# Norm statistics, norm and first projections of a stage by token segment in a one-core transformer program

## The chip, the cores and the metric

One core of one Trainium2 chip runs the whole program. The metric is the device time of one execution in microseconds: 2895.19 us as the median of three runs of the kernel before (2885.41 to 2896.55). Less is better.

## What is computed

Two transformer blocks of two and three layers run one after the other over 256 tokens of `x` and 256 tokens of a context `ctx`, width 1024. Every layer has a mixer and a feed-forward part, and each is entered through the same three steps: an RMS norm over the 1024 features, a scale and a shift that come from a modulation vector, and a projection. Each ends with an output projection that is added to `x` (and to the context) through a gate. In the reference this is:

```python
def rms_norm(x, g):
    xf = x.astype(jnp.float32)
    y = xf * lax.rsqrt(jnp.mean(xf * xf, axis=-1, keepdims=True) + EPS)
    return (y * g.astype(jnp.float32)).astype(x.dtype)
...
        hx = modulate(rms_norm_2(x, norm_ffn_g[i]), mod_x[3], mod_x[4])
        x = x + mod_x[5] * squared_relu_ffn(hx, ffn_w1[i], ffn_w2[i])
        if with_ctx_out:
            ctx = ctx + mod_c[2] * yc
            hc = modulate(rms_norm_2(ctx, norm_ffn_g[i]), mod_c[3], mod_c[4])
            ctx = ctx + mod_c[5] * squared_relu_ffn(hc, ffn_w1[i], ffn_w2[i])
```

The first block's mixers are a mixture of Fourier mixing, differential attention, neighbourhood attention and a gated MLP, followed by a convolutional feed-forward part. The second block's mixers are a gated delta rule, gated linear attention and plain attention, followed by a squared-ReLU feed-forward part.

## The kernel before

Activations lie with the features on the partitions: `xT` and `cT` are [128, 8, 256], feature 128k + p in partition p of slice k, one column a token. They stay in SBUF. A tile of 512 columns holds x's tokens in columns 0 to 255 and the context's in 256 to 511; these two halves are called segments. Every f32 operand is split into a high and a low part, and a product is three matmuls: high by high, low by high, high by low (`mm3`, L144 to L146). The weights come as [128, 1024] blocks by DMA into `raw`; ACT copies the high part (`whi`, L132) and POOL, or now and then DVE, subtracts it for the low part (`wlo`, L135). Two pairs of them rotate in one pool, and a third lies in the stage's own pool.

The stages, with the seams between them in the trace: start → mixer 0 (to 61 us), mixer 0 → FFN 0 (343), FFN 0 → mixer 1 (742), mixer 1 → FFN 1 (about 940), FFN 1 → delta mixer (1180), delta → ffn2(0) (2057), ffn2(0) → gla mixer (2425), gla → ffn2(1) (2690). FFN 1 and ffn2(1) have x only.

A seam consists of these pieces. `out_proj` (L666, for FFN stages) and `out_pair` (L800, for mixers) compute the eight output tiles of 128 features, 512 columns at a time. DVE adds each tile through the gate to `xT` and then to `cT` (L675, L811), and after a tile they call `stats`' step (L615 to L651) for the slice two tiles back, after the last tile for the last ones. A step squares the slice on ACT for x and for the context (L633); steps 1 to 5 are summed on DVE into `nsum` (L647); the sum, step 6 and step 7 go through matmuls with a matrix of ones that add over the partitions (L638, L635); then ACT takes Ln for both segments and Exp for both (L642, L645), which gives the reciprocal root. Ln and Exp each have an `ACT_TABLE_LOAD` before them. `norm_mod` (L651) makes from it the normed input of the next stage, slice by slice: on DVE `nt` = x · gain · `nsum` (L662), on ACT the high part `hh` = `nt` + shift (L663), on DVE the low part `hl` (L664). `nt` has two buffers. It goes over the eight slices, with the two segments inside. `first_fm` (L160), the mixers' `mix_first` (items at L1000) and the delta mixer's own list (L1479) send the next stage's first two or three projections through `mm3_lag` (L156 to L158), which takes slice after slice, all the items in each, the third item three slices later, so that PE can follow the norm while it goes on.

At the seams generators for the modulation vectors run in between (`mod_part`, L533). They either sum weight blocks `graw` by DVE into `gacc` (L547, L549) or take them through small matmuls (`bank_pm`, L552), then copy the result on ACT (`modt`, L564) and transpose it (L567).

The order on each engine is set by a scheduler that goes by the order of the code and by its own estimate of when operands are there. Each stage takes its tiles from pools that are opened at its start; their memory is that of the stage before, so that a first write into a new stage's tile waits for the last use of the old one.

## Time and profile before

| what | value |
|---|---|
| median of three runs | 2895.19 us (2885.41 to 2896.55) |
| profiled execution, its own time | 2895.47 us |
| its span, first to last instruction | 2893.7 us |
| mean granted TensorE clock | 0.972 of full speed |
| PE busy | 94%, 18,780 matmuls |
| PE weight loads busy | 72% |
| DVE, ACT, POOL busy | 60%, 45%, 35% |
| HBM read | 330.69 MB, 115 GB/s over the span |

The profile is that of one execution. Busy time of PE is counted from a matmul's start to its modelled end, and successive matmuls overlap, so the spacing of their starts is what a matmul costs in a dense stretch. The granted clock tells how much of the full speed of 2.4 GHz the chip gave TensorE in a stretch; the low level is 1.2 GHz.

### The profile page before, as it was taken

The page shows a single profiled execution, that of the slowest core. Times are in us where ns is not written, and L with a number is a line of the kernel's source. Part 1 is how long each engine was busy: PE and PEld are TensorE (multiplying, and loading weights), DVE is VectorE, ACT ScalarE, POOL GpSimd, SP SyncE. Part 2 cuts the span into 40 slices and gives each one's busy share as a digit, 9 for nine tenths or more (in the row PEclk, how much of TensorE's full clock was granted, in tenths as well). Part 3 has the DMA queues.
Part 4 walks back from the last instruction along what each step waited for, and adds up shares of the span by engine and source line. Part 5 has one row for each costly group of instructions (what it writes and reads, how often), then busy time and mean ns, then how long its engine had stood idle before and what let it go on. Part 6 is the DMA issues. An engine that isn't in the chain of part 4 may idle for free. (4 is left out here: it accounts for less than half of the span.)

```text
span 2893.7 us, 47135 instructions
## 1 busy us (share of the span) xinstructions
PE 2721.3 (94%) x18780; PEld 2085.7 (72%) x18780; DVE 1725.8 (60%) x3440; ACT 1302.6 (45%) x2287; POOL 1013.5 (35%) x565
## 2 busy tenths in 40 slices
...
GB/s 307 124 107 55 150 155 182 153 156 117 202 108 110 212 223 219 131 66 31 30 38 38 37 45 38 45 38 37 104 191 179 95 97 114 126 74 30 124 184 160
DMA packets 92567, 334.79 MB, mean 116 GB/s; under 512 B 10267, under 2 KB 10779, under 8 KB 91708
## 3 DMA queue, kind: packets, MB, share of 16 engines
...
HBM read 330.69 MB, written 1.05 MB: 115 GB/s over the span
## 5 line engine op out<-in xcount | busy, mean ns | idle before, releaser
L135 POOL TENSOR_TENSOR wlo<-raw,whi 128x1024 fp32r<-128x1024 f32 (+1 forms) x349 | 845.7, 2425 | 1732.8 <-ACT whi L132 1550.5
L132 ACT ACTIVATE whi<-raw 128x1024 fp32r<-128x1024 f32 (+1 forms) x418 | 437.3, 1046 | 691.9 <-PE bank_pj L145 429.6
L144 PE MATMUL bank_pj<-hh,whi 128*128 128x512 f32 (+1 forms) x1712 | 615.5, 360 | 1.7 <-DVE gz L1114 0.9
L146 PE MATMUL bank_pj<-hh,wlo 128*128 128x512 f32 (+1 forms) x1712 | 610.4, 357 | 5.6 <-POOL wlo L135 5.3
L145 PE MATMUL bank_pj<-hl,whi 128*128 128x512 f32 (+1 forms) x1712 | 609.0, 356 | 0.0
L146 PEld LDWEIGHTS bank_pj<-hh,wlo 128*128 128x128 f32 x1712 | 327.9, 192 | 62.0 <-issue 19.2
L144 PEld LDWEIGHTS bank_pj<-hh,whi 128*128 128x128 f32 x1712 | 327.9, 192 | 61.3 <-issue 23.3
L145 PEld LDWEIGHTS bank_pj<-hl,whi 128*128 128x128 f32 x1712 | 328.3, 192 | 49.0 <-issue 15.5
L549 DVE SCALAR_TENSOR_TENSOR gacc<-graw,sv,gacc 128x1024 f32<-128x1024 f32 x84 | 147.0, 1753 | 43.2 <-DMA graw<-in_ada_w 23.5
L144 PE MATMUL bank_pj<-f2h,whi 128*128 128x512 f32 (+1 forms) x512 | 172.5, 337 | 0.0
L145 PE MATMUL bank_pj<-f2l,whi 128*128 128x512 f32 (+1 forms) x512 | 171.2, 334 | 1.2 <-DVE f2l L175 1.2
L146 PE MATMUL bank_pj<-f2h,wlo 128*128 128x512 f32 (+1 forms) x512 | 171.9, 336 | 0.0
L175 DVE TENSOR_TENSOR f2l<-f2r,f2h 128x512 fp32r<-128x512 f32 (+1 forms) x64 | 66.5, 1044 | 126.9 <-ACT f2h L174 126.9
L144 PE MATMUL bank_pj<-acth,whi 128*128 128x512 f32 (+1 forms) x352 | 120.3, 343 | 7.9 <-ACT acth L174 7.9
L145 PE MATMUL bank_pj<-actl,whi 128*128 128x512 f32 (+1 forms) x352 | 119.0, 338 | 0.5 <-DVE actl L175 0.5
L146 PE MATMUL bank_pj<-acth,wlo 128*128 128x512 f32 (+1 forms) x352 | 119.1, 338 | 0.0
L675 DVE SCALAR_TENSOR_TENSOR xT<-bank_pj,m,xT 128x256 f32<-128x256 f32 x64 | 30.9, 483 | 141.7 <-PE bank_pj L146 141.6
L764 PE MATMUL bank_pj<-whi,hh 128*128 128x256 f32 x384 | 112.2, 292 | 1.3 <-DVE gck L1073 1.2
L764 PE MATMUL bank_pj<-wlo,hh 128*128 128x256 f32 x384 | 111.3, 290 | 1.4 <-POOL wlo L135 1.4
L764 PE MATMUL bank_pj<-whi,hl 128*128 128x256 f32 x384 | 111.0, 289 | 0.0
L552 PE MATMUL bank_pm<-graw,sv 128*32 128x256 f32 x896 | 81.9, 414 | 30.6 <-DMA graw<-in_w_ada 21.3
L145 PEld LDWEIGHTS bank_pj<-f2l,whi 128*128 128x128 f32 x512 | 96.0, 188 | 12.1 <-DVE f2l L175 1.4
...
## 6 DMA issues: line engine op xcount, KB each, us to landing
raw<-in_f SPq DMA_DIRECT2D x128, 512.0 KB, 3.7
graw<-in_w_ada SPq DMA_DIRECT2D x96, 512.0 KB, 4.5
graw<-in_ada_w SPq DMA_DIRECT2D x96, 512.0 KB, 4.5
raw<-in_up SPq DMA_DIRECT2D x88, 512.0 KB, 3.7
raw<-in_dn_w SPq DMA_DIRECT2D x48, 512.0 KB, 3.6
raw<-in_down SPq DMA_DIRECT2D x32, 512.0 KB, 3.6
raw<-in_win_fm SPq DMA_DIRECT2D x20, 512.0 KB, 3.8
raw<-in_win_tm SPq DMA_DIRECT2D x16, 512.0 KB, 5.1
```

The lines of the kernel that those rows point to most:

```text
L132: nc.scalar.activation(hi[:, :n], raw[:, :n], AF.Copy)
L135: eng.tensor_tensor(out=lo[:, :n], in0=raw[:, :n], in1=hi[:, :n].bitcast(F32), op=ALU.subtract)
L144: nc.tensor.matmul(out, lhsT=lh, rhs=rh, start=(idx == 0), stop=False)
L145: nc.tensor.matmul(out, lhsT=lh, rhs=rl, start=False, stop=False)
L146: nc.tensor.matmul(out, lhsT=ll, rhs=rh, start=False, stop=(idx == n - 1))
L175: nc.vector.tensor_tensor(out=lo, in0=src, in1=hi.bitcast(F32), op=ALU.subtract)
L549: nc.vector.scalar_tensor_tensor(out=acc[:, v], in0=raw, scalar=s[:, k, v:v + 1], in1=acc[:, v], op0=ALU.mult, op1=ALU.add)
L552: nc.tensor.matmul(ps[32 * j:32 * j + 32, :256], lhsT=s[:, k, :], rhs=raw[:, j * 256:(j + 1) * 256], start=first, stop=(k == 7 and direct ...
L675: nc.vector.scalar_tensor_tensor(out=x[:, mt], in0=ps[:, o:o + x.shape[2]], scalar=gate(vec, mt), in1=x[:, mt], op0=ALU.mult, op1=ALU.add)
L764: nc.tensor.matmul(out[i], lhsT=x, rhs=y, start=(a == 0 and kk == 0 and n == 0), stop=(a == 1 and kk == 3 and n == 2))
```

## The change

Segments get an order of their own at the seams, x's tokens first and the context's after them.

- `out_proj`: where statistics follow and there are two segments, the last three output tiles (5 to 7) are computed for x's 256 columns first, then for the context's; their three weight pairs are held meanwhile. `out_pair`: the second weight's four tiles (4 to 7) likewise.
- `stats`' step takes the segments it is for, and Squares, sums, ones matmuls, Ln and Exp are then made for those alone; Ln is one instruction over both where both are done together.
- `norm_mod` has the segments outside and the slices inside. A buffer `nt` is taken for one slice of one segment.
- The first projections run `mm3_lag` twice, over 256 columns of x and then of the context.

In all 463 matmuls of 512 columns become two of 256: 288 in first projections (72, 72, 24, 48 and 72 of them at the start, mixer 0 → FFN 0, FFN 0 → mixer 1, FFN 1 → delta and delta → ffn2(0)), 54 and 72 in output tiles of FFN 0 and ffn2(0), 24 + 24 in those of mixer 0 and delta. ACT gets eight more table loads, two at each of the four seams with two segments and statistics in the tiles. Outside of the seams the code is the same.

```diff
--- before.py
+++ after.py
@@ -153,17 +153,17 @@
...
     def first_fm(self, ws, h, T, tags, lags):
 
-        items = []
-        for (wh, wl), tag, lag in zip(ws, tags, lags):
-            items.append((self.bank(tag)[:, :T], [((wh[:, k], wl[:, k]), tuple(a[:, :T] for a in h(k))) for k in range(8)], lag))
-        self.mm3_lag(items)
-        return [i[0] for i in items]
+        banks = [self.bank(tag)[:, :T] for tag in tags]
+        for o in range(0, T, 256):
+            self.mm3_lag([(b[:, o:o + 256], [((wh[:, k], wl[:, k]), tuple(a[:, o:o + 256] for a in h(k))) for k in range(8)], lag)
+                          for b, (wh, wl), lag in zip(banks, ws, lags)])
+        return banks
 
@@ -616,45 +616,44 @@
 
 
         nc = self.nc
-        T = sum(x.shape[2] for x, _, _ in segs)
         st = {}
-        def step(k):
-            if k == 0:
+
+        def step(k, which=None):
+
+            some = [(i, x, o, o + x.shape[2]) for i, (x, _, o) in enumerate(segs) if which is None or i in which]
+            if not st:
                 st["ps"] = self.bank(bank)
-                self.rs = st["sum"] = sq = self.cp.tile([P, 512], F32, tag="nrs", name="nsum", bufs=1)
-            else:
-                sq = pool.tile([P, 512], F32, tag=tags[k % len(tags)], name="nsq", bufs=bufs)
-            ps = st["ps"]
+                self.rs = st["sum"] = self.cp.tile([P, 512], F32, tag="nrs", name="nsum", bufs=1)
+            ps, total = st["ps"], st["sum"]
+            ones = lambda x, o, e, start, stop: nc.tensor.matmul(ps[:, o:e], lhsT=self.c["ones"], rhs=x[:, o:e], start=start, stop=stop, skip_group_check=True)
             pr = self.tc.cur_priority
             if k >= 6:
                 self.tc.cur_priority = pr - PRI
-            for x, _, o in segs:
-                e = o + x.shape[2]
+            sq = total if k == 0 else pool.tile([P, 512], F32, tag=tags[k % len(tags)], name="nsq", bufs=bufs)
+            for i, x, o, e in some:
                 nc.scalar.activation(sq[:, o:e], x[:, k], AF.Square)
                 if k == 7:
-                    nc.tensor.matmul(ps[:, o:e], lhsT=self.c["ones"], rhs=sq[:, o:e], start=False, stop=True, skip_group_check=True)
+                    ones(sq, o, e, False, True)
+            lo, hi = some[0][2], some[-1][3]
             if k == 6:
-                for n, t in enumerate((st["sum"], sq)):
-                    nc.tensor.matmul(ps[:, :T], lhsT=self.c["ones"], rhs=t[:, :T], start=(n == 0), stop=False, skip_group_check=True)
+                ones(total, lo, hi, True, False)
+                ones(sq, lo, hi, False, False)
             if k == 7:
-                for x, _, o in segs:
-                    e = o + x.shape[2]
-                    nc.scalar.activation(self.rs[:, o:e], ps[:, o:e], AF.Ln, scale=1.0 / 1024, bias=self.const_col(EPS))
-                for x, _, o in segs:
-                    e = o + x.shape[2]
-                    nc.scalar.activation(self.rs[:, o:e], self.rs[:, o:e], AF.Exp, scale=-0.5)
+                nc.scalar.activation(total[:, lo:hi], ps[:, lo:hi], AF.Ln, scale=1.0 / 1024, bias=self.const_col(EPS))
+                for i, x, o, e in some:
+                    nc.scalar.activation(total[:, o:e], total[:, o:e], AF.Exp, scale=-0.5)
             if 0 < k < 6:
-                nc.vector.tensor_tensor(out=st["sum"][:, :T], in0=st["sum"][:, :T], in1=sq[:, :T], op=ALU.add)
+                nc.vector.tensor_tensor(out=total[:, lo:hi], in0=total[:, lo:hi], in1=sq[:, lo:hi], op=ALU.add)
             self.tc.cur_priority = pr
         return step
 
     def norm_mod(self, pool, segs, gs, m, part, dst, o0=0, tag="nt"):
 
         nc = self.nc
-        for k in range(8):
-            hi, lo = dst(k)
-            tt = pool.tile([P, 512], F32, tag=tag, name="nt", bufs=2)
-            for x, vec, o in segs:
+        for x, vec, o in segs:
+            for k in range(8):
+                hi, lo = dst(k)
+                tt = pool.tile([P, 512], F32, tag=tag, name="nt", bufs=2)
                 T = x.shape[2]
                 e = o + T
                 sh = m[:, part, vec, k:k + 1]
@@ -665,18 +664,33 @@
 
     def out_proj(self, w_ap, kt, act, segs, gate, tag="pj", after=None):
 
-        nc = self.nc
-        T = sum(x.shape[2] for x, _, _ in segs)
-        for mt in range(8):
-            wh, wl = self.weights(w_ap[mt], kt, P)
-            ps = self.bank(tag)[:, :T]
-            self.mm3(ps, [((wh[:, k], wl[:, k]), act(k)) for k in range(kt)])
-            for x, vec, o in segs:
-                nc.vector.scalar_tensor_tensor(out=x[:, mt], in0=ps[:, o:o + x.shape[2]], scalar=gate(vec, mt), in1=x[:, mt],
-                                               op0=ALU.mult, op1=ALU.add)
-            if after:
-                for k in ([mt - LAG] if mt >= LAG else []) + (list(range(8 - LAG, 8)) if mt == 7 else []):
-                    after(k)
+        def part(w, mt, which):
+            some = [segs[i] for i in which]
+            lo, hi = some[0][2], some[-1][2] + some[-1][0].shape[2]
+            ps = self.bank(tag)[:, lo:hi]
+            self.mm3(ps, [((w[0][:, k], w[1][:, k]), tuple(a[:, lo:hi] for a in act(k))) for k in range(kt)])
+            self.add_gated(ps, mt, some, gate, lo)
+            self.steps(after, mt, which, len(segs))
+        both = list(range(len(segs)))
+        cut = 5 if after and len(segs) == 2 else 8
+        for mt in range(cut):
+            part(self.weights(w_ap[mt], kt, P), mt, both)
+
+        last = [self.weights(w_ap[mt], kt, P) for mt in range(cut, 8)]
+        for i in both:
+            for mt in range(cut, 8):
+                part(last[mt - cut], mt, [i])
+
+    def add_gated(self, ps, mt, segs, gate, o0=0):
+        for x, vec, o in segs:
+            self.nc.vector.scalar_tensor_tensor(out=x[:, mt], in0=ps[:, o - o0:o - o0 + x.shape[2]], scalar=gate(vec, mt), in1=x[:, mt],
+                                                op0=ALU.mult, op1=ALU.add)
+
+    def steps(self, after, mt, which, n):
+
+        if after:
+            for k in ([mt - LAG] if mt >= LAG else []) + (list(range(8 - LAG, 8)) if mt == 7 else []):
+                after(*((k,) if len(which) == n else (k, which)))
...
@@ -799,21 +813,19 @@
 
     def out_pair(self, w_ap, y, segs, gate, tag="pj", after=None):
 
-        nc = self.nc
-        T = sum(x.shape[2] for x, _, _ in segs)
         for hf in range(2):
             wh, wl = self.weights(w_ap[hf], 2, 512)
-            for q in range(4):
-                mt = 4 * hf + q
-                ps = self.bank(tag)[:, :T]
-                self.mm3(ps, [((wh[:, k, q * P:(q + 1) * P], wl[:, k, q * P:(q + 1) * P]), y[k]) for k in range(2)])
-                for x, vec, o in segs:
-                    nc.vector.scalar_tensor_tensor(out=x[:, mt], in0=ps[:, o:o + x.shape[2]], scalar=gate(vec, mt), in1=x[:, mt],
-                                                   op0=ALU.mult, op1=ALU.add)
-                if after:
-                    for k in ([mt - LAG] if mt >= LAG else []) + (list(range(8 - LAG, 8)) if mt == 7 else []):
-                        after(k)
-                yield
+            both = list(range(len(segs)))
+            for which in ([[i] for i in both] if after and hf else [both]):
+                some = [segs[i] for i in which]
+                lo, hi = some[0][2], some[-1][2] + some[-1][0].shape[2]
+                for q in range(4):
+                    mt = 4 * hf + q
+                    ps = self.bank(tag)[:, lo:hi]
+                    self.mm3(ps, [((wh[:, k, q * P:(q + 1) * P], wl[:, k, q * P:(q + 1) * P]), tuple(a[:, lo:hi] for a in y[k])) for k in range(2)])
+                    self.add_gated(ps, mt, some, gate, lo)
+                    self.steps(after, mt, which, len(segs))
+                    yield
...
@@ -998,9 +1010,10 @@
 
         items = []
         for (i, tag, lag), (wh, wl) in zip(((0, "pj", 0), (2, "pj", 0), (1, "sc", 3)), W["first"]):
-            n = T if i < 2 else 512
-            items.append((self.bank(tag)[:, :n], [((wh[:, k], wl[:, k]), tuple(a[:, :n] for a in h(k))) for k in range(8)], lag))
-        self.mm3_lag(items)
+            items.append((self.bank(tag)[:, :T if i < 2 else 512], wh, wl, lag))
+        for o in (0, 256):
+            self.mm3_lag([(b[:, o:o + 256], [((wh[:, k], wl[:, k]), tuple(a[:, o:o + 256] for a in h(k))) for k in range(8)], lag)
+                          for b, wh, wl, lag in items if o < b.shape[1]])
...
@@ -1476,15 +1489,12 @@
             v.tensor_scalar(out=ng, in0=s_["dn_ng"], scalar1=0.5, scalar2=None, op0=ALU.mult)
             taps = s_["taps"].rearrange("p (h m t) -> p h m t", h=8, m=4)
             G = {}
-            items = []
-            wh, wl = ws[0]
-            for q in (1, 0):
-                hq = lambda k: tuple(t[:, q * 256:(q + 1) * 256] for t in h(k))
-                items.append((K.bank("pi")[:64, :256], [((wh[:, k], wl[:, k]), hq(k)) for k in range(8)], 0))
-            for n in range(2):
-                wh, wl = ws[1 + n]
-                items.append((K.bank("pj"), [((wh[:, k], wl[:, k]), h(k)) for k in range(8)], 3 * n))
-            K.mm3_lag(items)
+            items = [(K.bank("pi")[:64, :256], None, None)] + [(K.bank("pj"), None, None) for n in range(2)]
+            items.insert(0, (K.bank("pi")[:64, :256], None, None))
+            for q in range(2):
+                part = lambda k: tuple(t[:, q * 256:(q + 1) * 256] for t in h(k))
+                K.mm3_lag([(b, [((wh[:, k], wl[:, k]), part(k)) for k in range(8)], lag) for b, (wh, wl), lag in
+                           zip([items[1 - q][0]] + [i[0][:, q * 256:(q + 1) * 256] for i in items[2:]], ws, (0, 0, 3))])
...
```

What this does to the order of the instructions is seen at three places. The first is ACT at ffn2(0) → gla, from the last Squares (`nsq`) to the first normed activations (`hh`, of x). Before, and then in the changed kernel:

```order
L633 ACTIVATE nsq<-cT 128x256
L633 ACTIVATE nsq<-xT 128x256
L633 ACTIVATE nsq<-cT 128x256
L642 ACT_TABLE_LOAD
L642 ACTIVATE nsum<-bank_pf,cc_142 128x256 x2
L645 ACT_TABLE_LOAD
L645 ACTIVATE nsum<-nsum 128x256 x2
L132 ACTIVATE whi<-raw 128x1024
L663 ACTIVATE hh<-nt,m_1_88 128x256 x6
```

```order
L644 ACT_TABLE_LOAD
L644 ACTIVATE nsum<-nsum 128x256
L132 ACTIVATE whi<-raw 128x256
L634 ACTIVATE nsq<-cT 128x256
L132 ACTIVATE whi<-raw 128x1024
L634 ACTIVATE nsq<-cT 128x256 x2
L642 ACT_TABLE_LOAD
L642 ACTIVATE nsum<-bank_pf,cc_142 128x256
L132 ACTIVATE whi<-raw 128x1024
L644 ACT_TABLE_LOAD
L644 ACTIVATE nsum<-nsum 128x256
L662 ACTIVATE hh<-nt,m_1_88 128x256 x6
```

x's own Exp (the first two rows; its Ln stands two rows earlier) is now among the context's Squares; behind it come the context's last three Squares, its Ln, a weight's `whi`, its Exp, and only then x's first six `hh`.

The second is DVE at delta → ffn2(0), from the last add to the output tiles into the norm (`gacc`, a weighted sum for a modulation vector, waits for a DMA). Before, and then in the changed kernel:

```order
L811 SCALAR_TENSOR_TENSOR cT<-bank_pj,m_0_87,cT 128x256
L611 SCALAR_TENSOR_TENSOR gs<-m_0_87,smalls 128x16 [waits PE_49,Pool_49]
L662 SCALAR_TENSOR_TENSOR nt<-xT,gs,nsum 128x256 [waits DVE_49,Activation_49]
L662 SCALAR_TENSOR_TENSOR nt<-cT,gs,nsum 128x256 [waits Activation_49]
L662 SCALAR_TENSOR_TENSOR nt<-xT,gs,nsum 128x256
L547 TENSOR_SCALAR gacc<-graw,sv_82 128x1024 [waits DMAHW7_49]
L664 SCALAR_TENSOR_TENSOR hl<-nt,m_0_87,hh 128x256 [waits Activation_49] x2
L549 SCALAR_TENSOR_TENSOR gacc<-graw,sv_82,gacc 128x1024 [waits DMAHW0_49,DVE_49]
L664 SCALAR_TENSOR_TENSOR hl<-nt,m_0_87,hh 128x256 [waits Activation_49]
L662 SCALAR_TENSOR_TENSOR nt<-cT,gs,nsum 128x256
L662 SCALAR_TENSOR_TENSOR nt<-xT,gs,nsum 128x256 [waits DVE_49]
L662 SCALAR_TENSOR_TENSOR nt<-cT,gs,nsum 128x256
```

```order
L686 SCALAR_TENSOR_TENSOR cT<-bank_pj,m_0_87,cT 128x256 [waits PE_49]
L646 TENSOR_TENSOR nsum<-nsum,nsq 128x256 [waits DVE_49,Activation_49] x2
L611 SCALAR_TENSOR_TENSOR gs<-m_0_87,smalls 128x16 [waits PE_49,DVE_49,Activation_49,Pool_49]
L661 SCALAR_TENSOR_TENSOR nt<-xT,gs,nsum 128x256 [waits DVE_49]
L661 SCALAR_TENSOR_TENSOR nt<-xT,gs,nsum 128x256
L663 SCALAR_TENSOR_TENSOR hl<-nt,m_0_87,hh 128x256 [waits Activation_49] x2
L661 SCALAR_TENSOR_TENSOR nt<-xT,gs,nsum 128x256 [waits DVE_49] x2
L663 SCALAR_TENSOR_TENSOR hl<-nt,m_0_87,hh 128x256 [waits Activation_49]
L547 TENSOR_SCALAR gacc<-graw,sv_82 128x1024 [waits DMAHW7_49]
L663 SCALAR_TENSOR_TENSOR hl<-nt,m_0_87,hh 128x256 [waits Activation_49]
L661 SCALAR_TENSOR_TENSOR nt<-xT,gs,nsum 128x256 [waits DVE_49] x2
L549 SCALAR_TENSOR_TENSOR gacc<-graw,sv_82,gacc 128x1024 [waits DMAHW0_49]
```

x's `nt` still stand behind the context's last add, and from the second pair on each pair of `nt` and `hl` has a `gacc` in it, to the end of the norm: seven, where before there were four. At mixer 0 → FFN 0 there are now nine, where before there were four.

The third is PE at ffn2(0) → gla in the changed kernel, where x's last output tile ends and the context's first one begins (`bank_pf` <- `nsum`, `nsq` are the ones matmuls for x):

```order
L145 MATMUL bank_pj<-f2l,whi 128x256
L146 MATMUL bank_pj<-f2h,wlo 128x256
L144 MATMUL bank_pj<-f2h,whi 128x256
L628 MATMUL bank_pf<-nsum,base 128x256
L145 MATMUL bank_pj<-f2l,whi 128x256
L628 MATMUL bank_pf<-nsq,base 128x256 x2
L146 MATMUL bank_pj<-f2h,wlo 128x256
L144 MATMUL bank_pj<-f2h,whi 128x256
L145 MATMUL bank_pj<-f2l,whi 128x256
```

Before, the ones matmuls stood behind the last output tile; x's now stand behind one and two matmuls of the context's first tile (5), and everything of that tile stands behind them.

## Rows read from the trace of the kernel before

**Rows 1.** Busy time by stretch: PE, PEld, DVE, ACT, POOL; clock, DMA share, GB/s.

```profile
0.00:61.00 61.00, 37.81 (x248) 20.46 (x249) 24.30 (x70) 24.55 (x51) 1.44 (x5) 0.92 0.85 318
343.00:378.00 35.00, 25.99 (x117) 18.14 (x116) 26.77 (x50) 16.93 (x33) 4.95 (x2) 0.80 0.43 139
742.00:769.00 27.00, 19.44 (x109) 13.89 (x107) 19.22 (x47) 17.03 (x32) 6.17 (x3) 0.87 0.73 261
...
1218.00:2057.00 839.00, 798.94 (x7073) 517.07 (x7073) 625.60 (x1437) 425.54 (x877) 282.08 (x238) 0.99 0.14 41
2057.00:2088.00 31.00, 23.85 (x85) 17.25 (x84) 22.67 (x44) 17.71 (x34) 6.85 (x3) 0.83 0.48 158
2425.00:2458.00 33.00, 24.04 (x157) 20.30 (x155) 21.58 (x42) 19.86 (x34) 7.33 (x3) 0.90 0.44 135
```

**Rows 2.** What ended PE's idle time before L156: us, times.

```profile
  ACT hh L663: 52.3, 15
```

**Rows 3.** PE's timeline, ffn2(0) → gla: start, us, operation, [idle <-releaser].

```profile
2425.64 0.40 PE L146 MATMUL bank_pj<-f2h,wlo 128*128 128x512 f32 x1
...
2432.99 0.42 PE L156 MATMUL bank_gp<-hh,whi 128*32 128x256 f32 x1 [4.37 <-ACT hh L663]
```

**Rows 4.** Timeline of ACT, the same seam.

```profile
2427.42 1.28 ACT L642 ACT_TABLE_LOAD   x1
2428.71 0.84 ACT L642 ACTIVATE nsum<-bank_pf,cc 128x256 f32<-128x256 f32 x2
...
2430.86 0.72 ACT L645 ACTIVATE nsum<-nsum 128x256 f32<-128x256 f32 x2
2431.49 1.04 ACT L132 ACTIVATE whi<-raw 128x1024 fp32r<-128x1024 f32 x1
2432.44 0.89 ACT L663 ACTIVATE hh<-nt,m 128x256 fp32r<-128x256 f32 x2
```

**Rows 5.** Timeline of DVE, the same seam.

```profile
2426.47 0.48 DVE L675 SCALAR_TENSOR_TENSOR cT<-bank_pj,m,cT 128x256 f32<-128x256 f32 x1
...
2432.97 2.67 DVE L664 SCALAR_TENSOR_TENSOR hl<-nt,m,hh 128x256 fp32r<-128x256 f32 x2 [0.77 <-ACT hh L663]
2435.56 0.87 DVE L662 SCALAR_TENSOR_TENSOR nt<-xT,gs,nsum 128x256 f32<-128x256 f32 x2
...
2437.41 0.87 DVE L662 SCALAR_TENSOR_TENSOR nt<-xT,gs,nsum 128x256 f32<-128x256 f32 x2
```

**Rows 6.** Timeline of POOL, the same seam.

```profile
2432.61 2.35 POOL L135 TENSOR_TENSOR wlo<-raw,whi 128x1024 fp32r<-128x1024 f32 x1 [8.68 <-ACT whi L132]
```

**Rows 7.** PE's timeline in dense stretches, 256 and 512 columns.

```profile
1101.00 0.28 PE L144 MATMUL bank_pj<-hh,whi 128*128 128x256 f32 x1
1101.12 0.28 PE L145 MATMUL bank_pj<-hl,whi 128*128 128x256 f32 x1
...
2200.24 0.39 PE L145 MATMUL bank_pj<-hl,whi 128*128 128x512 f32 x1
2200.47 0.39 PE L146 MATMUL bank_pj<-hh,wlo 128*128 128x512 f32 x1
```

**Rows 8.** DVE's timeline, FFN 0 → mixer 1: first and last of 12 `hl`.

```profile
754.93 0.47 DVE L664 SCALAR_TENSOR_TENSOR hl<-nt,m,hh 128x256 fp32r<-128x256 f32 x1
...
763.64 0.47 DVE L664 SCALAR_TENSOR_TENSOR hl<-nt,m,hh 128x256 fp32r<-128x256 f32 x1
```

**Rows 9.** Timeline of ACT, the same seam.

```profile
743.87 1.06 ACT L132 ACTIVATE whi<-raw 128x1024 fp32r<-128x1024 f32 x1 [5.36 <-DMA raw<-in_win_fm]
```

**Rows 10.** Timeline of PE, mixer 0 → FFN 0.

```profile
357.27 0.69 PE L567 MATMUL bank_pm<-base,modt 128*128 128x128 f32 x2 [4.06 <-ACT modt L564]
```

**Rows 11.** DVE's timeline, delta → ffn2(0): two sums in the norm.

```profile
2068.68 1.27 DVE L549 SCALAR_TENSOR_TENSOR gacc<-graw,sv,gacc 128x1024 f32<-128x1024 f32 x1
...
2071.94 1.29 DVE L549 SCALAR_TENSOR_TENSOR gacc<-graw,sv,gacc 128x1024 f32<-128x1024 f32 x1 [0.40 <-DMA graw<-in_ada_w]
```

**Rows 12.** DMA issues: count, KB each, us from issue to landing.

```profile
graw<-in_ada_w SPq DMA_DIRECT2D x96, 512.0 KB, 4.5
```

6 lines of the change are left out of this document (3 added, 3 removed).

## The prediction

> **What bounds the kernel now.** I read the page first, whose shares stand in the table above: PE is busy for 94% of the span, no other engine for more than 60%, and the chain that ended last runs through PE lines only. So a change counts if it fills or makes PE's idle time, adds to PE's work, or alters the clock PE is granted. The change touches the seams between stages, so the second view is the table of stretches, one row a seam [rows 1]. The reader is to see there that seams are the bad places: at mixer 0 → FFN 0 (343 to 378) PE is busy 25.99 of 35 us at a mean granted clock of 0.80, at FFN 0 → mixer 1 19.44 of 27 at 0.87, at delta → ffn2(0) 23.85 of 31 at 0.83, at ffn2(0) → gla 24.04 of 33 at 0.90. Idle there: 9.0 + 7.6 + 7.2 + 9.0 = 32.8 us. The third view says for whom PE waits: in front of the first projections' first product (L156) it stood 52.3 us for the normed activations `hh`, 15 times [rows 2].
>
> The fourth view is the seam itself, engine by engine. At ffn2(0) → gla the last output matmul starts at 2425.64 and the first projection at 2432.99, 7.35 us later [rows 3]. Between them one thing follows another: the adds (the second at 2426.47, 0.48 us, [rows 5]), Squares, the ones matmuls, a table load of 1.28 us, Ln (two in 0.84), a second table load, Exp (two in 0.72), one weight's `whi` (1.04), then `hh` at 2432.44 [rows 4]. Then PE starts and stops again: the first two `hl` take 2.67 us instead of about 0.88 [rows 5], while POOL's `wlo` runs from 2432.61 to 2434.96 [rows 6]; the two read SBUF side by side and the `hl` ends only after the `wlo`. From there DVE sets the pace.
>
> **What the change could bring, and does not.** If x's statistics and norm ran under the context's last output tiles, PE would pass from the context's tiles to x's projections without a pause. Whether they do is settled by the order on ACT and DVE, whose rows in the trace come in the order of the program. In the order of the changed kernel x's Ln and Exp do come early, but x's first `hh` stands behind the context's own Squares, table load, Ln, a `whi`, table load and Exp, at all four seams; on DVE x's first `nt` stands behind the context's last add. That `nt` also needs the new stage's memory, which the old stage frees with its last statistics matmul. So PE still ends its last output tile, now a context tile, with nothing to do until a chain like the old one is through.
>
> **The sum, by parts.** It is made against the profiled execution, 2895.47 us (0.3 over the median of 2895.19).
>
> *More matmuls.* 463 matmuls of 512 columns become two of 256. Starts are 0.23 us apart at 512 columns and 0.12 at 256 [rows 7], so a split costs 0.01 us, 4.6 us if PE bound everywhere. Only the output tiles are PE-bound (54 + 72 + 48 of them, 1.7 us); the 288 in the first projections have the norm's pace as cover, and without it would cost 2.9.
>
> *ffn2(0) → gla.* The chain loses one add (0.48), one Ln (0.42) and one Exp (0.36) [rows 4, 5]: −1.2. The third weight's `whi` moves ahead of the context's second table load and Exp, so its `wlo` starts some 2 us (1.28 + 0.72) sooner against `hh`, and is done when `hl` comes: −1.8 (2.67 − 0.88). Against that x's three ones matmuls stand two matmuls into the context's first tile; PE waits there for x's tile 7 to be added (0.48) and squared (about as an Ln, 0.42): +0.9. 72 splits: +0.7. The norm here went by segment before. Sum **−1.5**; ends −4 and +1.5.
>
> *FFN 0 → mixer 1.* The same −1.2 and +0.9, and 0.5 for 54 splits. x's norm comes first and needs 8 steps, not 16 interleaved ones, before x's projections can be read, but each step gets slower: with both segments in turn an `hl` came every 0.79 us (8.71 us for 11 steps, [rows 8]), with one segment alone a pair of steps took 1.85, so 0.925 each [rows 5]: two `nt` buffers are then two steps, and DVE waits for ACT. Over 16 steps that is +2.2. The gain is that a wait for a late weight, 5.36 us of ACT before its `whi` [rows 9], and small loads of that stage fall under the context pass: −1 to −7, taken as −4.9. Sum **−2.5**; ends −5 and +1.6.
>
> *Mixer 0 → FFN 0.* Here the first projections wait for modulation matmuls: PE stood 4.06 us for `modt` from ACT [rows 10], which stood behind `hh`, which stood for a DVE busy with weighted sums `gacc`. In the new order `modt` stands behind four `hh` of x that need no such sum: the start comes about 4 us sooner. But nine `gacc` of 1.27 us [rows 11] now stand in the norm, where four stood: 9 × 1.27 + 8 × 1.85 = 26.2 us from the first `nt`, and some 7.3 us until then, 33.5 where the stretch had 35.0 [rows 1]. Sum **−1.5**; ends −4 (the earlier start is all kept) and +2.5 (two more sums' worth lost).
>
> *Delta → ffn2(0).* Chain −1.2 and `wlo` −1.8 as above, but seven of the eight pairs now carry a `gacc`, where four did: 7 × 1.27 + 8 × 1.85 = 23.7 us from the first `nt`. With some 6.8 us until that `nt`, 30.5 us, where the stretch had 31.0 [rows 1]. Sum **−0.5**; ends −4 and +4.
>
> *FFN 1 → delta and start → mixer 0.* Only the norm's order and the splits: up to +2.2 each by the two paces. At the start DMA is 0.85 busy [rows 1] and hides half: **+1** (0 to 2.2). At delta the third weight is late anyway: **+1.5** (0 to 2.2).
>
> *The delta mixer.* The order of its 839 us is shuffled by 10 to 25 places on DVE with the same work in it. It has 40 us of PE idle (839.00 − 798.94, [rows 1]); a tenth of it either way is my bound: **0** ± 4.
>
> Sum −1.5 − 2.5 − 1.5 − 0.5 + 1 + 1.5 = −3.5, so 2892.0 against the profiled execution and 2891.7 against the median: I say **2892**. The parts' ends do not all fall together; half of each summed gives about −13 and +9.
>
> The eight added table loads stand in none of these terms: x's two at each seam run while PE has context tiles, 2.9 us of them at the least (24 × 0.12). The Trainium skill's page ScalarE: Activation LUTs, section Table sets: the hidden batching unit, asks to batch activations by set, and speaks against this change. The trace agrees on the price, 1.28 us a load [rows 4]. It is a rival below.
>
> **Rivals.** *A, the overlap works.* The seams' idle time of 32.8 us would go, and PE busy time of 26.0, 19.4, 23.9 and 24.0 us would run at the full clock instead of 0.80, 0.87, 0.83 and 0.90: 5.2 + 2.5 + 4.1 + 2.4 = 14.2 more. Two thirds of 47 is −31: 2864. For it: x's statistics really end sooner. Against it: the order of `hh` and `nt`; in the trace each engine's rows come in its program's order, so the `hh` cannot pass the Exp ahead of it. The Trainium skill's page Perfetto Trace Analysis, section Optimizing Scalar/DVE Operations, holds that breaking up instructions may let work complete sooner where an engine causes bubbles; this is what it would then do. Chance 0.12, mild forms past −14.5 counted in.
>
> *B, the sums in the norm starve.* Each `gacc` waits for a weight block, 4.5 us from issue to landing [rows 12]. In the old seam two came 3.26 us apart, 0.40 of it waiting [rows 11]. With two buffers in flight a block can come every 2.9 us ((4.5 + 1.27) / 2), just under the 3.1 (1.85 + 1.27) that a pair needs. If the blocks come one at a time, every 4.5 us, seven pairs lose 1.4 each: +10 at delta → ffn2(0), +7 at mixer 0 → FFN 0, with PE waiting at the low clock meanwhile. With the other terms at the bad half of their ends: 2911. It decides from a landing pace above 3.1 us. For it: DMA is 0.43 and 0.48 busy there and the sum stands in front of `hl` on an in-order engine. Against: the 3.26 above. Chance 0.08.
>
> *C, the table loads show.* At the two seams with only four context tiles of six matmuls (2.9 us) x's chain of two loads, Ln and Exp (3.3 us) delays the context's Squares; with all eight loads on the path it is 8 × 1.28 = 10.3 on top of my sum: 2902. Chance 0.10, within the bound of no change.
>
> **How the numbers follow.** A measurement of this kernel can tell a change from none at about 0.5%, 14.5 us, so from 2880.7 to 2909.7 is no change. My forecast has 0.70, C 0.10, A 0.12, B 0.08. Forecast and C lie inside the bound except for 0.01 at each end. Faster 0.13, same 0.78, slower 0.09. The forecast's own range is 2879 to 2901; with C and a share of A and B, to leave out 2 in 10 or less, 2876 to 2907.
>
> **What would show it.** Right: ACT still runs the context's Exp before x's first `hh`; the pause from the last output matmul to the first projection is some 6 to 8 us at the three last two-segment seams; the `hl` right after x's first `hh` take 0.88 a pair; DVE's norm at delta → ffn2(0) shows pairs 3.1 us apart; 0.9 us of PE waiting at x's ones matmuls. Wrong: a seam with under 3 us of PE idle (A), `gacc` rows with several us of waiting for DMA (B), or the delta mixer longer or shorter than 839 us by more than 4.

## The result, and the profile after

The changed kernel takes 2926.95 us, the median of six runs (2919.79 to 2934.5), against 2895.87 for the kernel before (six runs): a ratio of 1.0111, 95% interval 1.0083 to 1.0139. The prediction was 2892 with a range to 2907, and slower by over 0.5% had a chance of 0.09: it was wrong.

The profiled execution took 2932.31 us, 36.8 more than that of before. The busy time of the changed kernel on the page (share of the span, instructions), and its granted clock:

```profile
PE 2745.8 (94%) x19258; PEld 2129.0 (73%) x19258; DVE 1734.6 (59%) x3454; ACT 1314.4 (45%) x2293; POOL 1007.1 (34%) x565
```

```profile
core 0: 2930.5 us, clock 0.967
```

PE is busy 94% of a longer span and its clock is lower, 0.967 for 0.972: by the page alone everything has become a little worse. What ended PE's idle time before the matmuls of L156 (us, times):

```profile
  ACT hh L662: 19.1, 7
  DMA consts<-in_k_gla: 4.2, 1
```

The kernel before has 24.6 us there, 7 times, for `hh`. The 52.3 us of [rows 2] are more than PE's own waits: they add those of the weight loads of the same line (27.7 us, 8 times), which lie in front of the same matmuls. `consts` was issued at 2466.63 us and landed 4.7 us later, when this product had been running since 2470.33; the weight load that starts with it waited for `hh`. So 23.3 us stand where 24.6 stood: the wait that the change was aimed at is still there, and has not grown. The growth must be read place by place. The same instruction's start in the two traces, one minus the other, gives for each stage how far the changed kernel has fallen behind:

| place | predicted, us | grew by, us |
|---|---|---|
| start → mixer 0 | +1 | −0.3 |
| mixer 0 → FFN 0 | −1.5 | +6.6 |
| FFN 0 → mixer 1 | −2.5 | +3.1 |
| inside mixer 1, and mixer 1 → FFN 1 | none | −0.6 |
| FFN 1 → delta | +1.5 | +3.6 |
| inside the delta mixer | 0 ± 4 | **+16.0** |
| delta → ffn2(0) | −0.5 | +7.9 |
| ffn2(0) → gla | −1.5 | +1.5 |
| behind it | none | −0.9 |

Two entries make two thirds of it: a mixer whose code behind its entry has not changed, and delta → ffn2(0). The row mixer 0 → FFN 0 holds mixer 0 itself, too. Each entry is that of one execution; e1 below shows how much the first ones differ in another.

**The delta mixer.** It is taken here from PE's first matmul on `gg` (L212) to DVE's add of x's output tile 4. (In the changed kernel this tile is only 256 columns wide and its add comes some 0.6 us sooner: up to the add before it, that of the context's tile 3, the mixer grew by 16.6 and delta → ffn2(0) by 7.3.) The table of stretches for it, before and then in the changed kernel (columns as in [rows 1]):

```profile
1225.47:2052.43 826.96, 789.00 (x7031) 509.88 (x7032) 614.31 (x1421) 418.69 (x866) 274.95 (x236) 0.99 0.13 40
```

```profile
1237.85:2080.85 843.00, 794.93 (x7030) 512.52 (x7030) 623.87 (x1419) 417.82 (x864) 272.40 (x235) 0.98 0.13 39
```

The reader is to see that the work is the same (7,031 matmuls and 7,030) and the time is not: 826.96 and 843.00 us, with 38.0 and 48.1 us of PE idle, and PE busy 5.9 us longer at a clock of 0.98 for 0.99. For whom PE waits in this stretch (us in total, times, longest), before and then in the changed kernel:

```profile
PE bank_pc L509 <- DVE o L504: 6.8, 6, 2.2
...
PE bank_pc L445 <- DVE S L487: 3.5, 10, 0.6
```

```profile
PE bank_pc L509 <- DVE o L504: 14.6, 8, 2.2
PE bank_pc L445 <- DVE S L487: 5.3, 9, 2.3
...
PE bank_pf L144 <- DVE rnt L297: 3.3, 2, 2.9
```

DVE has the same rows in another order, and PE waits for it more. PE, ACT and POOL have their rows in another order there, too. Below, DVE's order stands for that of the whole stage; which engine's order costs the time was not tried.

**Delta → ffn2(0).** The seams as stretches, in the changed kernel (mixer 0 → FFN 0, FFN 0 → mixer 1, delta → ffn2(0), ffn2(0) → gla; answers to [rows 1]):

```profile
345.00:381.00 36.00, 28.54 (x179) 22.16 (x180) 25.42 (x51) 14.48 (x28) 2.36 (x1) 0.76 0.43 135
749.00:779.00 30.00, 21.52 (x150) 17.49 (x150) 20.45 (x47) 15.37 (x29) 9.42 (x4) 0.86 0.68 237
2091.00:2124.00 33.00, 25.22 (x163) 21.99 (x164) 24.44 (x46) 17.82 (x33) 5.72 (x3) 0.84 0.58 177
2463.00:2496.00 33.00, 24.33 (x164) 21.51 (x164) 20.24 (x41) 19.75 (x32) 9.35 (x4) 0.90 0.46 149
```

Three of these stretches are 1 to 3 us longer than those of [rows 1]. Idle time (7.5, 8.5, 7.8 and 8.7 us) and clock are close to those of before, the clock at the first seam apart, 0.76 for 0.80. Much of the growth lies ahead of these stretches, in the tiles by segment. DVE's timeline in the changed kernel at delta → ffn2(0), over x's tiles:

```profile
2079.45 0.68 DVE L646 TENSOR_TENSOR nsum<-nsum,nsq 128x512 f32<-128x512 f32 x1
...
2081.24 2.96 DVE L646 TENSOR_TENSOR nsum<-nsum,nsq 128x256 f32<-128x256 f32 x2
2084.12 0.87 DVE L686 SCALAR_TENSOR_TENSOR xT<-bank_pj,m,xT 128x256 f32<-128x256 f32 x2
2084.91 0.94 DVE L646 TENSOR_TENSOR nsum<-nsum,nsq 128x256 f32<-128x256 f32 x2
```

POOL's timeline there:

```profile
2081.01 2.38 POOL L135 TENSOR_TENSOR wlo<-raw,whi 128x1024 fp32r<-128x1024 f32 x1 [15.70 <-ACT whi L132]
```

PE's timeline there:

```profile
2084.65 0.41 PE L144 MATMUL bank_pj<-yh,whi 128*128 128x256 f32 x1 [1.94 <-DVE xT L686]
...
2087.00 1.05 PE L628 MATMUL bank_pa<-nsum,base 128*128 128x256 f32 x2
2087.84 1.25 PE L628 MATMUL bank_pa<-nsq,base 128*128 128x256 f32 x4
...
2094.29 0.70 PE L628 MATMUL bank_pa<-nsum,base 128*128 128x256 f32 x2 [2.58 <-DVE nsum L646]
```

Two sums of 256 columns take 0.94 us, but 2.96 beside POOL's `wlo`, which ends at 2083.39. The Trainium skill's page SBUF — State Buffer, section SBUF: two separate sides, says that a DVE operation with two SBUF inputs and a GpSimd operation that reads SBUF exclude each other for a whole instruction; these rows agree. Both of x's next adds stand behind the two sums, and PE's next tile waits 1.94 us for the first of these to free its PSUM bank. Then x's ones matmuls (1.7 us, 2087.00 to 2088.7) stand in the context's first tile. The collision itself is not new: in the kernel before, one sum of 512 columns stood beside a `wlo` at this place, and PE waited behind it. DVE's and then PE's timeline before:

```profile
2053.22 2.11 DVE L647 TENSOR_TENSOR nsum<-nsum,nsq 128x512 f32<-128x512 f32 x1
```

```profile
2056.26 0.47 PE L144 MATMUL bank_pj<-yh,whi 128*128 128x512 f32 x1 [1.07 <-DVE cT L811]
```

PE's last wait above, 2.58 us for `nsum`, has another origin. ACT's and then DVE's timeline in the changed kernel:

```profile
2091.23 1.28 ACT L644 ACT_TABLE_LOAD   x1
2092.52 0.42 ACT L644 ACTIVATE nsum<-nsum 128x256 f32<-128x256 f32 x1
2092.84 0.70 ACT L634 ACTIVATE nsq<-cT 128x256 f32<-128x256 f32 x2
```

```profile
2093.28 0.96 DVE L646 TENSOR_TENSOR nsum<-nsum,nsq 128x256 f32<-128x256 f32 x2 [1.03 <-ACT nsq L634]
```

Two of the context's Squares stand behind x's second table load and Exp, DVE's sum waits 1.03 us for them, and PE waits for the sum.

### The profile page after: what moved, and what is told of

It is laid out like the page before. It is cut to its first block, busy times and chain, and to the rows that moved or that the text cites. A ratio compares the mean times of both kernels' runs of the same rounds, so it can differ in the third digit from the quotient of the medians.

```text
span 2930.5 us, 48103 instructions
## 1 busy us (share of the span) xinstructions
PE 2745.8 (94%) x19258; PEld 2129.0 (73%) x19258; DVE 1734.6 (59%) x3454; ACT 1314.4 (45%) x2293; POOL 1007.1 (34%) x565
## 5 line engine op out<-in xcount | busy, mean ns | idle before, releaser
L686 DVE SCALAR_TENSOR_TENSOR xT<-bank_pj,m,xT 128x256 f32<-128x256 f32 x168 | 80.8, 482 | 193.1 <-PE bank_pj L146 192.7
L145 PE MATMUL bank_pj<-f2l,whi 128*128 128x256 f32 (+1 forms) x536 | 175.9, 328 | 1.2 <-DVE f2l L175 1.2
L144 PE MATMUL bank_pj<-f2h,whi 128*128 128x256 f32 (+1 forms) x536 | 176.4, 329 | 0.0
L146 PE MATMUL bank_pj<-f2h,wlo 128*128 128x256 f32 (+1 forms) x536 | 175.9, 328 | 0.0
L549 DVE SCALAR_TENSOR_TENSOR gacc<-graw,sv,gacc 128x1024 f32<-128x1024 f32 x84 | 137.6, 1640 | 41.6 <-DMA graw<-in_ada_w 21.4
L144 PE MATMUL bank_pj<-acth,whi 128*128 128x256 f32 (+1 forms) x370 | 123.5, 335 | 7.9 <-ACT acth L174 7.9
L145 PE MATMUL bank_pj<-actl,whi 128*128 128x256 f32 (+1 forms) x370 | 122.3, 331 | 0.5 <-DVE actl L175 0.5
L146 PE MATMUL bank_pj<-acth,wlo 128*128 128x256 f32 (+1 forms) x370 | 122.5, 331 | 0.0
```

Source lines behind the costliest of these rows:

```text
L144: nc.tensor.matmul(out, lhsT=lh, rhs=rh, start=(idx == 0), stop=False)
L145: nc.tensor.matmul(out, lhsT=lh, rhs=rl, start=False, stop=False)
L146: nc.tensor.matmul(out, lhsT=ll, rhs=rh, start=False, stop=(idx == n - 1))
L549: nc.vector.scalar_tensor_tensor(out=acc[:, v], in0=raw, scalar=s[:, k, v:v + 1], in1=acc[:, v], op0=ALU.mult, op1=ALU.add)
L686: self.nc.vector.scalar_tensor_tensor(out=x[:, mt], in0=ps[:, o - o0:o - o0 + x.shape[2]], scalar=gate(vec, mt), in1=x[:, mt], op0=ALU.mul ...
```

## The experiments

**e1: the delta mixer's entry as before.** The changed kernel, but the delta mixer's norm goes slice by slice and its first projections are 512 wide:

```diff
-                K.norm_mod(np_, segs, gs, M2[0], 0, h)
+                K.norm_mod(np_, segs, gs, M2[0], 0, h, by=False)
...
+            items = []
+            wh, wl = ws[0]
+            for q in (1, 0):
+                hq = lambda k: tuple(t[:, q * 256:(q + 1) * 256] for t in h(k))
+                items.append((K.bank("pi")[:64, :256], [((wh[:, k], wl[:, k]), hq(k)) for k in range(8)], 0))
+            for n in range(2):
+                wh, wl = ws[1 + n]
+                items.append((K.bank("pj"), [((wh[:, k], wl[:, k]), h(k)) for k in range(8)], 3 * n))
+            K.mm3_lag(items)
```

> The changed kernel, but the delta mixer is entered as before: its norm goes slice by slice over both segments, its first projections are 512 wide. In the order of its instructions the delta mixer is then row for row that of the kernel before. Theory A (most of the loss is the reshuffled order inside the delta mixer): the offset against the kernel before stays where it is at the mixer's entry, about +9 us, and does not grow by some 16 inside the mixer; the total falls from 2927 to about 2909. Theory B (the loss inside the mixer has another cause than its order, such as a lower granted clock or a lost transfer that the earlier seams bring about): the offset still grows by over 10 inside the mixer and the total stays above 2920.

Measured: 2906.03 us (ten runs, 2893.57 to 2922.82), ratio 1.0038 (1.0017 to 1.0059). DVE's rows in the delta mixer stand in the order of before again, and the mixer takes 829.99 us. This edit alone takes back 21 of the 31 us. Up to FFN 1 the program is that of the changed kernel, row for row; yet mixer 0 → FFN 0 cost +0.9 here (+2.2 without mixer 0 itself) and FFN 0 → mixer 1 −0.1, where the changed kernel's profile had +6.6 and +3.1. The stretch of 345 to 381 us shows a granted clock of 0.86 here and of 0.76 there (above). e2, below, is the same program up to FFN 1, too, and has +3.7 (without mixer 0) and +3.4.

**e2: a third order.** The changed kernel with 512-wide first projections in the delta mixer (the second half of e1's edit), its norm by segment. DVE's order in the mixer is then neither that of before nor that of the changed kernel.

> The changed kernel with the delta mixer's first projections 512 wide as before, but its norm by segment. The work inside the mixer is the same, the order of its instructions is a third one, neither that of before nor that of the change. Theory A (the order is what costs): the offset gained inside the mixer is neither 0 nor 16 us but some third value, anywhere from -5 to +30. Theory C (the two-pass projections at the entry are the cause, through what they make ready first): the offset inside the mixer is near 0, within 3 us, and the total is near 2911.

Measured: 2926.18 us (four runs, 2919.96 to 2930.59), ratio 1.0104 (1.0074 to 1.0134); the mixer takes 837.54 us, between the other two. A third order of the same work has a third price (its stretch holds 7,054 matmuls, as the first on `gg` stands a little sooner in it). The total says less here, as its profile lost 9 us to a low clock in mixer 0 (the last section has such a case).

**e3 and e9: output tiles by segment alone.** Norm and first projections as before:

```diff
-        for x, vec, o in segs:
-            for k in range(8):
-                hi, lo = dst(k)
-                tt = pool.tile([P, 512], F32, tag=tag, name="nt", bufs=2)
+        for k in range(8):
+            hi, lo = dst(k)
+            tt = pool.tile([P, 512], F32, tag=tag, name="nt", bufs=2)
+            for x, vec, o in segs:
...
+        items = []
+        for (wh, wl), tag, lag in zip(ws, tags, lags):
+            items.append((self.bank(tag)[:, :T], [((wh[:, k], wl[:, k]), tuple(a[:, :T] for a in h(k))) for k in range(8)], lag))
+        self.mm3_lag(items)
```

> Only the last output tiles and the statistics go by segment; norms and first projections are as before, and the delta mixer has the order of before row for row. Theory A: no growth inside the delta mixer; the four seams pay for the tiles (x's ones matmuls ahead of the context's tiles, adds behind locked sums), about +13 us in all, so about 2908. Theory D (the output tiles are free and the seams' loss is that of norm and projections): the four seams together lose under 4 us, total 2895 to 2900.

> e3's kernel a second time, beside e10 on the same chip: 2904 to 2910, and the stretch from the first output tile by segment to the first projection at delta -> ffn2(0) within 0.5 us of e3's 19.98.

Measured: e3 2907.49 us (ten runs, 2904.47 to 2919.23), ratio 1.0035 (1.0017 to 1.0052); e9, in another set of runs, 2916.25 (four runs, 2906.26 to 2924.9), ratio 1.0081 (1.0057 to 1.0105), above what was expected. The delta mixer has the order of before and takes 827.16 and 830.16 us. At the seams the two profiles agree far better than the medians. From DVE's add to `cT` of the last tile that is whole to the first projection, in us:

| seam | before | changed | e3, e9 | e7, e10 |
|---|---|---|---|---|
| mixer 0 → FFN 0 | 23.19 | 27.24 | 24.40, 24.62 | 24.22, 24.33 |
| FFN 0 → mixer 1 | 22.21 | 21.92 | 21.70, 21.70 | 24.51, 24.51 |
| delta → ffn2(0) | 14.42 | 20.42 | 19.98, 19.93 | 18.46, 18.50 |
| ffn2(0) → gla | 23.00 | 24.01 | 24.01, 24.02 | 26.50, 26.50 |

Tiles by segment cost 5.5 us at delta → ffn2(0), some 1 us at two seams, and gain 0.5 at one. The tiles take longer everywhere, the pause behind them gets shorter at three of the four. In e1 and e2, which have the changed kernel's program there, the first row is 24.23 and 24.17: the 27.24 of the changed kernel's profile holds 3 us of that one execution, with PE idle for 9 us in all three and a granted clock of 0.79, 0.87 (e1) and 0.93 (e2).

**e4: norm and first projections by segment alone.** The other half:

```diff
-        cut = 5 if after and len(segs) == 2 else 8
+        cut = 8
...
-            for which in ([[i] for i in both] if after and hf else [both]):
+            for which in ([[i] for i in both] if False else [both]):
```

> Only norms and first projections go by segment; output tiles and statistics are as before. The delta mixer has the order of the changed kernel row for row. Theory A: the offset grows by some 16 us inside the mixer, as in the changed kernel, and by 2 at its entry; the seams give about +5 together, total about 2917. Theory D: the seams lose as much as in the changed kernel, +15 together, total about 2927.

Measured: 2915.08 us (four runs, 2914.48 to 2916.93), ratio 1.0068 (1.0047 to 1.0089). DVE's order in the delta mixer is that of the changed kernel, row for row, and it takes 842.32 us. The seams: −0.9 at mixer 0 → FFN 0, +3.3 at FFN 0 → mixer 1, +3.4 at FFN 1 → delta, +3.7 at delta → ffn2(0), −2.4 at ffn2(0) → gla, where nothing but Ln differs from before (one instruction over both segments) and PE and DVE have their rows in the old order. The 40 us behind the seam's first 33 had a granted clock of 0.88 before and of 1.00 here. So the growth of one seam in one execution carries an error of some microseconds, as e1 showed too. At delta → ffn2(0) tiles alone (e3) cost 7.4, this half 3.7, both together 7.9 (6.3 in e1, 9.1 in e2): the halves do not add.

**e5: the order of the changed kernel without any work by segment.** The code of before in all of its work; only memory differs: the normed activations lie in a pool of their own, and `nt` has four slots of 256 columns.

```diff
-                tt = pool.tile([P, 512], F32, tag=tag, name="nt", bufs=2)
+        ring, j = self.wp.tile([P, 1024], F32, tag="raw", name="nt", bufs=self.RAW), 0
...
-                t = tt[:, o:e]
+                t = ring[:, 256 * (j % 4):256 * (j % 4) + T]
+                j += 1
...
-            h = halves(fp, T, 8, "h")
+            h = halves_x(T)
```

> The kernel before in all of its work (nothing by segment: tiles, statistics, norm and first projections are all as before), but the normed activations of every stage lie in memory that no other stage uses, and `nt` has four slices of 256 columns in one weight buffer. DVE's order in the delta mixer comes out as in the changed kernel, to a place or two, though nothing there is split. Theory A (the growth inside the delta mixer comes from the order alone): the delta mixer grows by 10 to 16 us against before although no segment work is there, the other seams stay within 3 us of before or gain by the freer memory; 2905 to 2915. Rival D (the growth comes from the work by segment at the delta mixer's entry): no growth in the delta mixer, 2890 to 2898.

Measured: 2913.17 us (six runs, 2909.22 to 2924.32), ratio 1.0076 (1.005 to 1.0102). The mixer takes 844.61 us. PE's waits in it:

```profile
PE bank_pc L509 <- DVE o L504: 14.6, 8, 2.2
PE bank_pc L445 <- DVE S L487: 6.1, 9, 2.3
...
PE bank_pa L212 <- DVE gg L204: 3.9, 1, 3.9
...
PE bank_pf L144 <- DVE rnt L297: 3.3, 2, 2.9
```

Nothing is split in this kernel, and two of these waits, the first and the last, are those of the changed kernel to the tenth. The wait for `gg` stands at the very beginning; the mixer begins 3.8 us sooner behind FFN 1 than before. So the entry and the mixer are best taken together, from x's last add in FFN 1 to the add to `cT` of tile 3: 870.82 us before, 890.76 in the changed kernel, 889.64 in e4, 884.63 here. The order without any work by segment costs 13.8 us of the changed kernel's 19.9; the 6 us between them lie in the entry (3.3 us longer in the changed kernel, 3.8 shorter here). What costs time in the delta mixer is the order of its rows and not the work by segment. All profiles of this study together:

| order of DVE's rows in the delta mixer | length, us |
|---|---|
| as before | 826.96 (before), 829.99 (e1), 827.16 (e3), 825.63 (e7), 827.53 (e8), 830.16 (e9), 826.37 (e10) |
| a third one | 837.54 (e2) |
| as in the changed kernel (e5, e6: but for its beginning, to a place) | 843.00 (changed), 842.32 (e4), 844.61 (e5), 843.63 (e6) |

**e6: an overlap that can happen.** e5's memory with tiles, statistics, norm and projections by segment (the delta mixer's entry as in e1). At ffn2(0) → gla all of x's `hh` now stand ahead of the context's Ln.

> The same memory with tiles, statistics, norm and first projections by segment, except that the delta mixer's entry is as before. The order in the delta mixer is that of e5. Now all eight of x's `hh` stand ahead of the context's Ln at ffn2(0) -> gla, three at delta -> ffn2(0), two at mixer 0 -> FFN 0, none at FFN 0 -> mixer 1, so an overlap is possible for the first time. Theory A (the pause was x's norm standing behind the context's statistics): at ffn2(0) -> gla the pause from the last output matmul to the first projection falls from 5.4 to under 3 us, at FFN 0 -> mixer 1 it stays at 6 to 8; a pair of `nt` and `hl` takes under 1.85 us with four slots; the tiles by segment still cost some 12 us, so the run is within 6 us of e5. The prediction's rival (an overlap that works takes the 32.8 us of idle time and the low clock away): 20 us or more below e5.

Measured: 2920.19 us (five runs, 2911.88 to 2925.73), ratio 1.0088 (1.0056 to 1.0121), 7 over e5, where at most 6 either way had been expected. x's norm really runs under the context's tiles: ACT's timeline at ffn2(0) → gla:

```profile
2447.25 0.51 ACT L663 ACTIVATE hh<-nt,m 128x256 fp32r<-128x256 f32 x1 [1.07 <-DVE nt L662]
...
2454.88 0.42 ACT L634 ACTIVATE nsq<-cT 128x256 f32<-128x256 f32 x1 [3.14 <-DVE cT L687]
```

DVE's timeline there:

```profile
2451.02 3.36 DVE L664 SCALAR_TENSOR_TENSOR hl<-nt,m,hh 128x256 fp32r<-128x256 f32 x3
2454.31 0.47 DVE L687 SCALAR_TENSOR_TENSOR cT<-bank_pj,m,cT 128x256 f32<-128x256 f32 x1
```

PE's timeline there:

```profile
2449.98 0.28 PE L146 MATMUL bank_pj<-f2h,wlo 128*128 128x256 f32 x1
...
2455.34 1.22 PE L628 MATMUL bank_pf<-nsq,base 128*128 128x256 f32 x2 [4.05 <-ACT nsq L634]
2457.95 0.42 PE L156 MATMUL bank_gp<-hh,whi 128*32 128x256 f32 x1 [1.39 <-ACT nsum L642]
```

x's first `hh` starts 2.7 us ahead of the last output matmul, and yet the first projection comes 7.97 us behind that matmul (before: 7.35 [rows 3]). The context's last ones matmul stands ahead of x's projections in PE's queue, it waits for the context's last Square, that for the context's last add, and that stands on DVE behind x's `nt` and `hl`, three of which take 3.36 us beside POOL's `wlo` (2450.31 to 2453.31). By its row the projection then waits for the context's Ln as well. The pause under 3 us that I expected was wrong: what is done for x sooner makes the context later, and PE takes the context's matmul first. The Trainium skill's page PSUM — Partial Sum Buffer, section Engine vs sequencer instructions, has matmuls start in program order; here `hh` is there 10 us before PE comes to it. Four slots bring the 16th `hl` of FFN 0 → mixer 1 to 22.23 us behind the last output matmul (27.71 in the changed kernel, 22.62 before), but that seam did not get shorter by it (+2.4 in this profile): the end of the norm is not what PE waits for there.

**e7 and e10: the sums on PE.** e3's kernel, where a slice of a tile by segment goes through the ones matrix instead of DVE's add:

```diff
-            if k == 6:
+            alone = which is not None and k < 7
+            if alone:
+                if ("on", lo) not in st:
+                    st["on", lo] = ones(total, lo, hi, True, False) or True
+                ones(sq, lo, hi, False, False)
+            if k == 6 and not alone:
...
-            if 0 < k < 6:
+            if 0 < k < 6 and not alone:
```

> e3's kernel (output tiles by segment alone), with the sums of squares of the tiles by segment made by matmuls with the ones matrix on PE instead of adds on DVE: 28 more ones matmuls of 256 columns, no half-size `nsum` add on DVE. The order in the delta mixer stays as before. Theory A (the tiles by segment cost time because DVE's half-size adds stand beside POOL's `wlo` and hold up the adds to xT and cT, on which PE's PSUM banks wait): the rows of DVE at 2.9 us for two adds are gone, PE's waits for nsum, xT and cT inside the last tiles fall from some 5 to under 2 us at delta -> ffn2(0) and mixer 0 -> FFN 0, and what PE has to do more (about 3 us a seam) gives most of it back: 2902 to 2910. Rival E (the waits come from the tiles' own adds, whatever the sums): the waits stay and the ones matmuls come on top, 2913 to 2920.

> e7's kernel a second time, on the same chip as e9. If e7's 2919 was that of its work: 8 or more above e9 again. If it was the clock in mixer 0, where this kernel has the rows of e3 and its profile still lost 10 us: at most 5 above e9, since the stretches at the seams summed to 3.6 us more than e3's.

Measured: e7 2919.25 us (seven runs, 2904.66 to 2924.93), ratio 1.0075 (1.0046 to 1.0104); e10 2909.23 (eight runs, 2902.24 to 2921.74), ratio 1.0049 (1.003 to 1.0068), 7 below e9. By its time e7 fell to rival E, by its trace it did not, and e10 sides with the trace. PE's waits in the last tiles of delta → ffn2(0), all there are up to the first projection:

```profile
2077.47 0.70 PE L628 MATMUL bank_pa<-nsq,base 128*128 128x256 f32 x2 [0.40 <-ACT nsq L634]
...
2080.02 0.70 PE L628 MATMUL bank_pa<-nsq,base 128*128 128x256 f32 x2 [0.52 <-ACT nsq L634]
2086.11 1.22 PE L156 MATMUL bank_pj<-hh,whi 128*128 128x512 f32 x2 [5.39 <-ACT hh L667]
```

The waits for `nsum` and `xT` are gone, so they did come by way of DVE's half-size sums; what is left of the context's late Squares are the two short waits for `nsq`. It is worth 1.5 us at this seam (table above); at the two FFN seams, where no such wait was, the added matmuls cost 2.5 to 2.8.

**e8: own memory in the first block alone.** The kernel before with e5's edit up to FFN 1.

> The kernel before, with memory of its own for the normed activations and four slots for `nt` in the first block's stages alone (e5's edit up to FFN 1; nothing by segment anywhere). DVE's order in the delta mixer is row for row that of before. Theory A (the order in the delta mixer is what e5 lost by, and its freer memory was a gain before that): the 4 us that e5 gained between mixer 1 and FFN 1 stay, no growth in the delta mixer; 2889 to 2896. Rival F (the freer memory is what slows the delta mixer, or e5's gain was the clock of one execution): 2896 to 2910.

Measured: 2896.26 us (twelve runs, 2891.68 to 2908.25), ratio 1.0014 (0.9999 to 1.0029). The median lies at the border of the two ranges. The delta mixer takes 827.53 us: e5's memory ahead of it, the old order in it, no growth. (What e5's memory does inside the delta mixer itself is not tried by this; the changed kernel and e4 have the growth without that memory.) The trace keeps 3.3 us of e5's gain before the mixer, the median shows none; whether that gain is real stays open. No version of this study beats the kernel before.

## Why the prediction was wrong

- *The delta mixer, "a tenth of it either way is my bound: 0 ± 4".* This is the step that failed. I had seen that its rows were shuffled and bounded the price by a share of PE's idle time. It measured +16.0: 10 us more of idle PE, and 6 more of PE busy with the same matmuls at a lower clock, which the bound left out altogether. The cause shows from both sides: with work by segment elsewhere and the old order the mixer takes what it took (e1, e3), with the changed order and no work by segment it is as long as in the changed kernel (e5). It is the order of the whole stage; which engine's rows it is in stays open.
- *The tiles by segment at the delta mixer's end.* The sum had 0.01 us a split and 0.9 for x's ones matmuls. At delta → ffn2(0) it cost 5.5 (e3). Undercounted were DVE's sums beside POOL, 2.96 us where one sum had taken 2.11, with PE's wait for a PSUM bank behind them, 1.94 for 1.07, and the ones matmuls in the context's tile; missed were the context's Squares behind x's table load and Exp. In e3 the tiles ran at a granted clock of 0.84, where before it was 1.00. e7 shows 1.5 of it to be the sums; the split of the rest is read from rows, not tried.
- *Mixer 0 → FFN 0 and FFN 0 → mixer 1, −1.5 and −2.5.* The gains did not come: in the three executions of the same program there (the changed kernel, e1, e2) they cost +6.7, +2.2 and +3.7 (without mixer 0) and +3.1, −0.1 and +3.4. "The start comes about 4 us sooner" had its reason right, PE's wait for `modt` fell from 4.06 us [rows 10] to 0.50:

```profile
361.18 0.69 PE L567 MATMUL bank_pm<-base,modt 128*128 128x128 f32 x2 [0.50 <-ACT modt L564]
```

But the first projection stands 13.26 (e1) and 13.18 us (e2) behind the last output matmul where it had stood 15.73, so 2.5 sooner, and 16.27 in the changed kernel's profile, where PE was busy for 9.21 of these us at a granted clock of 0.65, in e1 for 6.76 at 0.77. And the tiles ahead of it take longer. The −4.9 for a late weight is not to be seen: in the changed kernel the 16th `hl` of FFN 0 → mixer 1 comes 5.1 us later than before.
- *FFN 1 → delta:* +3.6 for +1.5, the right sign. *ffn2(0) → gla:* +1.5, the bad end of the range given.
- *What held.* There is no overlap: the context's Exp stands before x's first `hh` at all four seams of the changed kernel. ffn2(0) → gla, ACT's and then PE's timeline:

```profile
2465.44 1.28 ACT L642 ACT_TABLE_LOAD   x1
2466.73 0.47 ACT L642 ACTIVATE nsum<-bank_pf,cc 128x256 f32<-128x256 f32 x1
2467.11 1.05 ACT L132 ACTIVATE whi<-raw 128x1024 fp32r<-128x1024 f32 x1
2468.17 1.28 ACT L644 ACT_TABLE_LOAD   x1
2469.46 0.42 ACT L644 ACTIVATE nsum<-nsum 128x256 f32<-128x256 f32 x1
2469.79 0.90 ACT L662 ACTIVATE hh<-nt,m 128x256 fp32r<-128x256 f32 x2
```

```profile
2464.11 0.28 PE L146 MATMUL bank_pj<-f2h,wlo 128*128 128x256 f32 x1
...
2470.33 0.30 PE L156 MATMUL bank_gp<-hh,whi 128*32 128x256 f32 x1 [4.16 <-DMA consts<-in_k_gla]
```

The pause is 6.22 us; 7.35 less 1.2 had been worked out [rows 3 to 5]. It is 7.17 and 9.45 at FFN 0 → mixer 1 and delta → ffn2(0), where 6 to 8 had been said, and the norm of the latter took 23.4 us from its first `nt` for 23.7. The first two `hl` took 0.94 or 0.95 us at three of the four seams, for 0.88 said; at FFN 0 → mixer 1 the first alone took 2.27 beside a `wlo`. The 0.9 us of waiting at x's ones matmuls did not come; they took 1.1 to 1.7 us of PE's time instead. Rival A fell, and in e6, where the overlap was there, it did not pay. Rival B fell: the sums there come 2.8 us apart, and none of the seven in the norm waits for its block:

```profile
2107.92 1.28 DVE L549 SCALAR_TENSOR_TENSOR gacc<-graw,sv,gacc 128x1024 f32<-128x1024 f32 x1
...
2110.71 1.28 DVE L549 SCALAR_TENSOR_TENSOR gacc<-graw,sv,gacc 128x1024 f32<-128x1024 f32 x1
```

Rival C put its price on the table loads. At ffn2(0) → gla x's two ran while PE had context tiles. At the two seams with four context tiles its mechanism is there: at delta → ffn2(0) the rows above end in a wait of PE of 2.58 us, at mixer 0 → FFN 0 DVE's sum waits 1.22 us for such a Square and PE 1.40 for the sum. What the loads alone cost there was not tried.

These parts fit the total: 16.0, 7.9 at delta → ffn2(0), 3.6 and 1.5 are 29 of the 31 us by which the medians differ. With +2.2 and −0.1, as in e1, the two first seams make it 31; with the changed kernel's own +6.6 and +3.1 it is 39, but that execution took 5.4 us more than the median.

Some readings and sums of the prediction were off without deciding it. The 52.3 us for `hh` count weight loads with the matmuls (24.6). The chain on the page covers 7% of the span and has lines of POOL, DVE and ACT in it, at 0% each, so it says little of the whole. The split matmuls are 462, by their own parts as by the traces. Half of the parts' ends, each counted from its own term, come to −8.8 and +10.8, so 2883 to 2903 and not 2879 to 2901; what was measured lies outside of both.

The text named the sign by which it would be wrong ("the delta mixer longer or shorter than 839 us by more than 4") but gave it no chance of its own. Taken as a rival, "the new order costs the delta mixer a few per cent", it would have carried the range some 17 us (2% of 839, a share chosen in hindsight) further up, to 2924, 3 us short of what was measured.
